# Token rows of the router: from the vector engine to the scalar engine and GpSimd

## The chip, the core and the metric

The program runs on one core of a Trainium2 chip. A core has a matrix engine (PE, TensorE; PEld is its weight loading), a vector engine (DVE), a scalar engine (ACT), GpSimd (POOL) and a queue engine (SP) that here issues nearly all DMA transfers. Each engine works through its own instructions in order and waits on semaphores for the others. The metric is the device time of one execution in microseconds (us); lower is better.

## The reference

Two layers over 256 latent and 256 context tokens of width 1024. Each layer is a norm with modulation, an input projection, three parallel token mixers, an output projection with a residual, and then the part that matters here, a mixture of experts behind a router:

```python
hl = modulate(rms_norm(x, norm2_g[i]), sh2, sc2)            # the token rows h (layer 0: context rows too)
gp = softmax(h @ w_group + b_group);  g_val, g_idx = top_k(gp, 1)
el = (h @ w_expert + b_expert) of the chosen group;  e_val, e_loc = top_k(el, 2)
e_w = softmax(e_val) * g_val
out[e] = (silu(xb @ w_gate[e]) * (xb @ w_up[e])) @ w_down[e]    # for the rows xb sent to expert e
x = x + g2 * (sum over the two experts of e_w * out)
```

32 experts, 1024 x 512 each, three matrices, all in float32, in both layers.

## The kernel before

`layer(l)` writes out both layers. Tokens lie in tiles of 128: NT = 4 tiles in layer 0 (latent and context), NT = 2 in layer 1 (latent only). Expert weights are streamed from HBM through a ring of SBUF places and a pool of 18 tiles of 128 x 1024 (`K4`); what can be loaded before the experts start is loaded early, and after that a place is filled again when PE has read it.

The stretch in question lies between the last residual add and the first expert product:

- `turned(t)`: PE transposes the scaled residual of tile t into a PSUM tile `ht` (pool `P2`, two buffers).
- `lg`, `gmx`, `first_max`, ... to `selb`: the routing steps, some twenty short DVE instructions in a chain: logits, best group, first and second expert, and a 0/1 choice per token and expert.
- `late_mod()`: a modulation product of a later layer, placed in the middle; PE multiplies (line 283, tile `pm`), ACT copies (lines 290 and 306), GpSimd adds (lines 307 to 312). Layer 1 has `own_rows()` at that place instead (PE transposes `xot`, ACT copies `xo`).
- `pp`: PE counts the choices (lines 1218 and 1220); `pos` (DVE, line 1223) is each token's place in its expert; `OH` (line 1303) the one-hot rows of the first four experts.
- `tokens(t)`: DVE makes `h` of tile t, `ht` times the token's norm factor `r2` plus the row `Brow`, in two instructions of 128 x 512 (line 1115); ACT rounds it to `hH` (line 1117). `low(t)`: DVE makes the rest `hL = h - hH` (line 1121).
- `keep_warm(8)`: eight products on PE with no use for their result.
- `gather_all(t)`: PE multiplies `hH` and `hL` of tile t by the one-hot rows (lines 1328 and 1329, tile `pg`); after the last tile the experts' inputs `xg` are complete and the expert products `pgu` (line 1371) start.

From line 1058 on, until `rorder.close()`, the order on PE, DVE, ACT and POOL is that of the code (`rorder`, a manual schedule); SP's order is that of the code throughout. Before the change tile 0's `h` comes right behind `selb` on DVE, and tiles 1 to 3 follow one by one, each behind its transposes, since `ht` has two buffers only.

Of the kernel before, what the change touches and what calls it, by code (L numbers as in the profile page):

```python
# [14 lines left out]
AF = mybir.ActivationFunctionType  # L15
OP = mybir.AluOpType
# [20 lines left out]
def trunk(ctx: ExitStack, tc: tile.TileContext, t_in, rope, out, cfg):  # L37
    nc = tc.nc
    pe, ve, sc, gp, sp = nc.tensor, nc.vector, nc.scalar, nc.gpsimd, nc.sync
# [14 lines left out]
    def K4(name, shape=(128, 1024), dt=F32):  # L54
        return k4.tile(list(shape), dt, tag="k4", name=name)

    def K2(name, shape=(128, 512), dt=F32, tag="t"):
        t = k2[tag].tile([shape[0], 256 if tag == "m" else 512], dt, tag="k2" + tag, name=name)
        n = int(np.prod(shape[1:]))
        t = t[:, :n]  # L60
        if len(shape) == 3:
            t = t.rearrange("p (a b) -> p a b", a=shape[1])
        elif len(shape) == 4:
            t = t.rearrange("p (a b c) -> p a b c", a=shape[1], b=shape[2])
        return t

    def P2(name, dt=F32):
        return ps2.tile([128, 2, 512], dt, tag="p2", name=name)

    def P1(name, dt=F32):  # L70
        return ps1.tile([128, 512], dt, tag="p1", name=name)
# [109 lines left out]
    for i in range(4):  # L181
        t = K4("xtok")
# [146 lines left out]
    def rstd(ssq, n, cnt, name):  # L329

        v = sm.tile([128, n], F32, name=name + "v")
        ve.tensor_scalar(v, ssq, 1.0 / cnt, EPS, op0=OP.mult, op1=OP.add)
        s = sm.tile([128, n], F32, name=name + "s")
        sc.activation(s, v, AF.Sqrt)
        r = sm.tile([128, n], F32, name=name + "r")
        ve.reciprocal(r, s)
        u = sm.tile([128, n], F32, name=name + "u")
        ve.tensor_tensor(u, r, r, op=OP.mult)
        ve.scalar_tensor_tensor(u, u, -0.5, v, op0=OP.mult, op1=OP.mult)
        ve.scalar_tensor_tensor(r, u, 1.5, r, op0=OP.add, op1=OP.mult)  # L340
        return r
# [124 lines left out]
    def layer(l):  # L466
        last = l == DEPTH - 1
        NT = 2 if last else 4
# [439 lines left out]
        def chunked(a):  # L908

            return a.rearrange("t (a p k) -> t a k p", a=2, k=4)  # L910

        def bcast_row(m, s, name, of=lambda a: a):

            t = K4(name)
            p = P2(name)
            for k in range(KC):
                pe.transpose(p[:, k // 4, (k % 4) * 128:(k % 4) * 128 + 128],
                             mod[l][:, m, k, s:s + 1].to_broadcast([128, 128]), ident)
            t_ = t if of is not chunked else t.rearrange("t (a k p) -> t a k p", a=2, k=4)
            sc.copy(t_, of(p.rearrange("p a b -> p (a b)")))  # L920
            return t
# [87 lines left out]
        def weights_of(pr, m, a, e):  # L1009
            return down(a, e, pr) if m == 2 else gate_up(m, a, e, pr)  # L1010
# [5 lines left out]
        def preload_k4(key=None):  # L1016
            key = key or keys.pop(0)
            src = weights_of(*key)
            n = src.shape[1] // 2
            t = []  # L1020
            for b in range(2):
                v = K4("wp", (128, n, src.shape[2]))
                sp.dma_start(v, src[:, n * b:n * b + n])
                t.append(v)
            pre[key] = t
# [27 lines left out]
        for c in order[cfg["wo1"]:]:  # L1053
            t = K4("wo2", (128, 2, 512), F32R)
# [6 lines left out]
        for s in range(NS):  # L1061
            t = K2("wrA", (128, KC, 64))
            gp.tensor_tensor(t, wr, amod[l][:, 1, :, s, None].to_broadcast([128, KC, 64]), op=OP.mult)
            wrA.append(t)
        Brow = []
# [26 lines left out]
        r2 = rstd(ps[:, :NT], NT, D, f"n2{NT}")  # L1092
# [7 lines left out]
        hH, hL, ht, hf = {}, {}, {}, {}  # L1100

        def turned(t, ks=range(KC)):

            if t not in ht:
                ht[t] = P2("ht")
            for k in ks:
                pe.transpose(ht[t][:, k // 4, (k % 4) * 128:(k % 4) * 128 + 128], U(k, 128 * t, 128), ident)

        def tokens(t):
            hf[t] = K4("h")  # L1110
            hH[t] = K4("hH", (128, 1024), F32R)
            p = ht[t].rearrange("p a b -> p (a b)")
            rows = lambda a: a.rearrange("t (a k p) -> t a k p", a=2, k=4)
            for a in range(2):
                ve.scalar_tensor_tensor(rows(hf[t])[:, a], chunked(p)[:, a], r2[:, t:t + 1], rows(Brow[t // 2])[:, a],
                                        op0=OP.mult, op1=OP.add)
            sc.copy(hH[t], hf[t])

        def low(t):
            hL[t] = K4("hL", (128, 1024), F32R)  # L1120
            ve.tensor_tensor(hL[t], hf[t], hH[t].bitcast(F32), op=OP.subtract)
# [3 lines left out]
            pe.transpose(plt[:, 128 * b:128 * b + 128], ls[:, 128 * b:128 * b + 128], ident)  # L1125
        turned(0, range(4, KC))
        turned(1)
        for _ in range(2):
            preload_k4()
        lg = rt.tile([128, 4, 36], F32, name="lg")[:, :NT]  # L1130
# [22 lines left out]
        def own_rows():  # L1153

            for t in range(2):
                xo.append(K4("xo"))
                for a in range(2):
                    p = P1("xot")
                    for k in range(4):
                        pe.transpose(p[:, 128 * k:128 * k + 128], xT[:, 4 * a + k, 128 * t:128 * t + 128], ident)  # L1160
                    sc.copy(xo[t][:, 512 * a:512 * a + 512], p)
# [21 lines left out]
            late_mod()  # L1183
        if last:
            own_rows()
        if last:

            for i in range(cfg["prex"]):
                key = keys.pop(0)
                src = weights_of(*key)  # L1190
                v = xT[:, 4 * i:4 * i + 4].rearrange("p k f -> p (k f)").rearrange("p (k f) -> p k f", f=src.shape[2])
                sp.dma_start(v, src)
                pre[key] = v
# [14 lines left out]
        def keep_warm(n):  # L1208

            p = P1("warm")  # L1210
            for _ in range(n):
                pe.matmul(p[:, 0:256], identb, masks.rearrange("p a b -> p (a b)"), start=True, stop=True)
# [5 lines left out]
                pe.matmul(pp[:, 32 * t:32 * t + 32], tri if u == t else onesb, selb[:, u, :], start=u == 0, stop=u == t)  # L1218
        for u in range(NT):
            pe.matmul(pp[:32, 128:130], selb[:, u, :], onesb[:, 0:2], start=u == 0, stop=u == NT - 1)  # L1220
        tokens(0)
        pos = rt.tile([128, 4, 32], F32, name="pos")[:, :NT]
        ve.scalar_tensor_tensor(pos, pp[:, :32 * NT].rearrange("p (t e) -> p t e", e=32), 1.0, sel, op0=OP.add, op1=OP.mult)

# [319 lines left out]
        onehot()  # L1544
        cnt = rt.tile([32, 1], F32, name="cnt")
        ve.tensor_copy(cnt, pp[:32, 128:129])
        if last:
            g2r = bcast_row(5, 0, "g2r")
        for t in range(1, NT):
            if t > 1:  # L1550
                turned(t)
            tokens(t)
            low(t - 1)
            keep_warm(8)
        low(NT - 1)
        for _ in range(cfg["pre"][l] - 2):
            preload_k4()
        for t in range(NT):
# [102 lines left out]
    for l in range(DEPTH):  # L1661
        layer(l)
# [46 lines left out]
```

## Time and profile before

| what | value |
|---|---|
| median of 3 runs | 1451.4 us (1450.96 to 1451.78) |
| the profiled execution | 1453.9 us, its span 1452.1 us |
| mean granted TensorE clock | 0.983 of full speed |
| PE busy | 1387.6 us, 96% |
| DVE, ACT, POOL busy | 42%, 27%, 5% |
| DMA | 481.86 MB, 332 GB/s mean over the span |

The profile is of one execution. The span runs from the first to the last instruction; what lies around it is 1.8 us. A busy PE is not a PE at its peak. The routing stretch of layer 0 lies at about 284 to 305 us, that of layer 1 at about 965 to 984 us.

### The profile page before, as it was taken

To read this page: it belongs to the slowest core of one execution; us is meant where nothing else is said; L and a number is where in the kernel's file an instruction comes from. 1 tells how busy PE (TensorE), PEld (TensorE's weight loads), DVE (VectorE), ACT (ScalarE), POOL (GpSimd) and SP (SyncE) were. 2 spreads that over 40 slices of the span, in tenths; PEclk is the share of its full clock that TensorE was granted. 3 is DMA by queue.
4 is the path that set the end of the run, shared out by engine and by line. 5 is a ranking of instruction groups with operands and counts; after the bars stand their busy time and mean duration, and the time that the engine had idled before them with its cause. 6 is when DMAs were issued, how large, how long until landed. Compare 5 with 4: busy or idle time off the path is not lost. (4 is left out here: it accounts for less than half of the span.)

```text
span 1452.1 us, 20461 instructions
## 1 busy us (share of the span) xinstructions
PE 1387.6 (96%) x8068; PEld 775.0 (53%) x8068; DVE 610.5 (42%) x1380; ACT 395.0 (27%) x954; POOL 76.3 (5%) x132
## 2 busy tenths in 40 slices
PE   6999999999999999999998998989999999999987
PEld 5777677755445544455434776783434343334332
DVE  3479974353323333233334679853222222122223
ACT  4454775331111111111112565652111111101112
POOL 1212000100000000000001110010000000000000
PEclk9999999999999999999998998999999999999999
DMA  9748303387999999999999591098999999999996
GB/s 352 284 160 292 120 1 133 151 361 315 387 422 417 421 417 417 422 416 419 405 415 388 192 323 44 24 399 326 392 422 421 421 421 422 421 421 419 421 417 255
DMA packets 97556, 481.86 MB, mean 332 GB/s; under 512 B 14084, under 2 KB 22560, under 8 KB 52400
## 3 DMA queue, kind: packets, MB, share of 16 engines
q1 hardware_dynamic: 96720, 478.79, 82.0%
q8 instruction: 66, 1.08, 0.3%
q10 hardware_dynamic: 464, 1.11, 0.2%
q0 software_dynamic: 272, 0.59, 0.1%
q14 instruction: 34, 0.28, 0.1%
HBM read 479.42 MB, written 1.05 MB: 331 GB/s over the span
## 5 line engine op out<-in xcount | busy, mean ns | idle before, releaser
L1371 PE MATMUL pgu<-we,xg 128*64 128x512 f32 x1728 | 403.7, 595 | 12.9 <-DMA we<-in_w_gate_dram 9.3
L1371 PEld LDWEIGHTS pgu<-we,xg 128*64 128x64 f32 x1728 | 132.4, 137 | 270.6 <-issue 223.1
L1425 PE MATMUL py<-we,actT 128*64 128x512 f32 x784 | 178.5, 596 | 0.7 <-ACT actT L1386 0.7
L1380 DVE SCALAR_TENSOR_TENSOR act<-pgu,ws,sil 128x512 f32<-128x512 f32 x32 | 24.0, 751 | 272.6 <-PE pgu L1371 239.5
L1264 DVE SCALAR_TENSOR_TENSOR xT<-pc,mod,xT 128x256 f32<-128x256 f32 x256 | 104.8, 476 | 53.1 <-PE pc L1261 52.5
L1318 ACT COPY xg<-pg 128x256 f32<-128x256 f32 x112 | 36.3, 376 | 296.7 <-PE pg L1314 296.7
L1425 PEld LDWEIGHTS py<-we,actT 128*64 128x64 f32 x784 | 55.4, 137 | 103.2 <-issue 99.9
L1272 DVE TENSOR_TENSOR xo<-xo,pc 128x512 f32<-128x512 f32 x62 | 39.8, 683 | 108.4 <-PE pc L1271 108.4
L1313 PE MATMUL pg<-OH,hH 128*128 128x256 f32 x336 | 83.3, 286 | 0.0
L1314 PE MATMUL pg<-OH,hL 128*128 128x256 f32 x336 | 82.1, 282 | 0.0
L645 DVE SCALAR_TENSOR_TENSOR ca<-gpad,cw,ca 128x512 f32<-128x512 f32 (+1 forms) x120 | 73.2, 610 | 0.7
L1313 PEld LDWEIGHTS pg<-OH,hH 128*128 128x128 f32 x336 | 63.9, 190 | 7.2 <-issue 5.7
L1314 PEld LDWEIGHTS pg<-OH,hL 128*128 128x128 f32 x336 | 64.1, 191 | 0.9
L283 PE MATMUL pm<-wm,scT 128*32 128x256 f32 (+1 forms) x896 | 61.3, 367 | 3.2 <-DMA wm<-in_w_mod_dram 3.1
L1287 DVE TENSOR_TENSOR Yg<-py,g2r 128x512 f32<-128x512 f32 x31 | 21.3, 688 | 100.7 <-PE py L1425 96.4
L1375 ACT ACTIVATE sil<-pgu 128x512 f32<-128x512 f32 x32 | 19.1, 598 | 163.3 <-PE pgu L1371 163.3
L1290 DVE TENSOR_TENSOR YL<-py,YH 128x512 fp32r<-128x512 f32 x32 | 22.1, 690 | 92.8 <-ACT YH L1289 92.8
L1289 ACT CAST YH<-Yg 128x512 fp32r<-128x512 f32 x31 | 19.1, 618 | 141.1 <-DVE Yg L1287 141.1
L1289 ACT CAST YH<-py 128x512 fp32r<-128x512 f32 x32 | 18.7, 585 | 139.0 <-PE py L1425 113.8
L1394 POOL CAST se<-ident 32x128 fp32r<-32x128 f32 x32 | 9.0, 284 | 886.0 <-PE pb L1395 886.0
L1260 PE MATMUL pc<-oht,YH 128*128 128x512 f32 x128 | 53.4, 417 | 1.2 <-ACT YH L1289 1.2
L1371 PE MATMUL pgu<-xT,xg 128*64 128x512 f32 x176 | 46.4, 618 | 5.5 <-DMA xT<-in_w_gate_dram 2.6
(431 smaller groups left out, 2203.5 us busy)
## 6 DMA issues: line engine op xcount, KB each, us to landing
we<-in_w_up_dram SPq DMA_DIRECT2D x102, 1024.0 KB, 10.0
we<-in_w_gate_dram SPq DMA_DIRECT2D x100, 1024.0 KB, 14.8
we<-in_w_down_dram SPq DMA_DIRECT2D x98, 1024.0 KB, 12.3
wm<-in_w_mod_dram SPq DMA_DIRECT2D x44, 1024.0 KB, 8.8
xT<-in_w_down_dram SPq DMA_DIRECT2D x14, 1024.0 KB, 16.2
xT<-in_w_gate_dram SPq DMA_DIRECT2D x10, 1024.0 KB, 19.8
xT<-in_w_up_dram SPq DMA_DIRECT2D x10, 1024.0 KB, 18.8
wp<-in_w_gate_dram SPq DMA_DIRECT2D x8, 1024.0 KB, 10.4
```

The costliest lines, as they stand in the source:

```text
L283: pe.matmul(p[0][32 * q:32 * q + 32], scT[:, kq, :], ws[128 * kq // nr][:, kq % (nr // 128), c:c + n], start=k == 0, stop=k == KC * nq // ...
L645: ve.scalar_tensor_tensor(a, g, wt, a, op0=OP.mult, op1=OP.add)
L1260: pe.matmul(pc, YH[:, 128 * o:128 * o + 128], oht, start=True, stop=False)
L1264: ve.scalar_tensor_tensor(xT[:, o, sl], pc[:, sl], mod[l][:, 5, o, s:s + 1], xT[:, o, sl], op0=OP.mult, op1=OP.add)
L1272: ve.tensor_tensor(xo[t][:, sl], xo[t][:, sl], pc, op=OP.add)
L1289: sc.copy(YH[:rows, sl], py)
L1313: pe.matmul(dst, hH[t][:, 128 * k:128 * k + 128], rhs, start=t == 0, stop=False)
L1314: pe.matmul(dst, hL[t][:, 128 * k:128 * k + 128], rhs, start=False, stop=t == NT - 1)
L1318: sc.copy(xg[e][:, k - 1:k + 1, :], v[:, :, e])
L1371: pe.matmul(p[64 * e:64 * e + 64, :], xg[:, k, 64 * e:64 * e + 64], w_[e](k % 4), start=k == 0, stop=k == KC - 1)
L1380: ve.scalar_tensor_tensor(act, p, ws, sil, op0=OP.mult, op1=OP.mult)
L1425: pe.matmul(py[64 * e:64 * e + 64, h], actT[:, 128 * f + 64 * e:128 * f + 64 * e + 64], wd[e](f % 2)[:, 512 * h:512 * h + 512], start=f == ...
```

## The change

`tokens` no longer makes `h`. A new function `scaled(t)` does: ACT multiplies `ht` by `r2` from PSUM into `h` (two instructions of 128 x 512), and GpSimd adds `Brow` to each half in place. Tiles 0 and 1 are scaled right behind their transposes, before the routing steps, and the transposes of tiles 2 and 3 come there too; tiles 2 and 3 are scaled behind `late_mod`. The rounding to `hH` follows for all tiles on ACT, and DVE makes the four `hL` behind `OH`. One `keep_warm(8)` is left where layer 0 had three (layer 1 had one and keeps it).

```diff
+        def scaled(t):
+
+            hf[t] = K4("h")
+            p = ht[t].rearrange("p a b -> p (a b)")
+            rows = hf[t].rearrange("t (a k p) -> t a k p", a=2, k=4)
+            for a in range(2):
+                sc.activation(rows[:, a], chunked(p)[:, a], AF.Identity, scale=r2[:, t:t + 1])
+                sl = slice(512 * a, 512 * a + 512)
+                gp.tensor_tensor(hf[t][:, sl], hf[t][:, sl], Brow[t // 2][:, sl], op=OP.add)
+
         def tokens(t):
-            hf[t] = K4("h")
             hH[t] = K4("hH", (128, 1024), F32R)
-            p = ht[t].rearrange("p a b -> p (a b)")
-            rows = lambda a: a.rearrange("t (a k p) -> t a k p", a=2, k=4)
-            for a in range(2):
-                ve.scalar_tensor_tensor(rows(hf[t])[:, a], chunked(p)[:, a], r2[:, t:t + 1], rows(Brow[t // 2])[:, a],
-                                        op0=OP.mult, op1=OP.add)
             sc.copy(hH[t], hf[t])
...
         turned(0, range(4, KC))
         turned(1)
+        for t in range(2):
+            scaled(t)
+        for t in range(2, NT):
+            turned(t)
...
         if last:
             own_rows()
+        for t in range(2, NT):
+            scaled(t)
+        for t in range(NT):
+            tokens(t)
...
-        tokens(0)
         pos = rt.tile([128, 4, 32], F32, name="pos")[:, :NT]
...
+        for t in range(NT):
+            low(t)
         if last:
             g2r = bcast_row(5, 0, "g2r")
-        for t in range(1, NT):
-            if t > 1:
-                turned(t)
-            tokens(t)
-            low(t - 1)
-            keep_warm(8)
-        low(NT - 1)
+        keep_warm(8)
```

DVE in layer 0 from the end of the routing steps, before (`rt` stands for the routing tables, `n24r` for `r2`; a name's number is left out):

```order
L1207 CAST selb<-rt 128x128
L1115 SCALAR_TENSOR_TENSOR h<-ht,n24r,Brow 128x512 x2
L1223 SCALAR_TENSOR_TENSOR pos<-pp,rt 128x128
L1303 TENSOR_TENSOR OH<-pos,i_108 128x512 x2
L1546 COPY cnt<-pp 32x1
L1115 SCALAR_TENSOR_TENSOR h<-ht,n24r,Brow 128x512 x2
L1121 TENSOR_TENSOR hL<-h,hH 128x1024
L1115 SCALAR_TENSOR_TENSOR h<-ht,n24r,Brow 128x512 x2
L1121 TENSOR_TENSOR hL<-h,hH 128x1024
L1115 SCALAR_TENSOR_TENSOR h<-ht,n24r,Brow 128x512 x2
L1121 TENSOR_TENSOR hL<-h,hH 128x1024 x2
```

The same place on DVE after the change:

```order
L1219 CAST selb<-rt 128x128
L1234 SCALAR_TENSOR_TENSOR pos<-pp,rt 128x128
L1314 TENSOR_TENSOR OH<-pos,i_108 128x512 x2
L1557 COPY cnt<-pp 32x1
L1125 TENSOR_TENSOR hL<-h,hH 128x1024 x4
```

The eight instructions that made `h` are gone from DVE; the routing steps ahead of `selb` stand as they were.

GpSimd in layer 0 after the change, from the sums of squares (line 977) to the first experts (line 1405, before 1394); before, lines 1117 were not there:

```order
L977 TENSOR_TENSOR sq<-sq 128x512 x5
L1117 TENSOR_TENSOR h<-h,Brow 128x512 x4
L307 TENSOR_TENSOR mod_224<-mod_224,va 128x16
L311 TENSOR_TENSOR amod_226<-mod_224,ones 128x16
L312 TENSOR_TENSOR amod_226<-amod_226,va 128x16
L1117 TENSOR_TENSOR h<-h,Brow 128x512 x4
L1405 CAST se<-ident 32x128 x12
```

Four adds came in ahead of the three small ones of `late_mod`, and four behind them; layer 1 has four in all.

ACT in layer 0 after the change, from the copy of the logits (`ls`) to the copies of the gathered rows (`xg`); before, only lines 1096, 290, 306 and the four roundings stood here:

```order
L1096 COPY ls<-pl 128x256
L1115 ACTIVATE h<-ht,n24r 128x512 x4
L290 COPY ms<-pm 128x256
L306 COPY mod_224<-pm 128x16
L1115 ACTIVATE h<-ht,n24r 128x512 x4
L1121 CAST hH<-h 128x1024 x4
L1344 COPY xg<-pg 128x256 x8
```

The second four scalings stand behind the two copies of `late_mod`, and all four roundings behind those.

## Rows read from the trace of the kernel before

**Rows 1.** The page, part 1: busy us, share of the span, instructions.
```profile
PE 1387.6 (96%) x8068; PEld 775.0 (53%) x8068; DVE 610.5 (42%) x1380; ACT 395.0 (27%) x954; POOL 76.3 (5%) x132
```

**Rows 2.** SP's waits, 240 to 320 us: total us, times, longest.
```profile
SPq L100 <- PE pgu L1371: 16.9, 3, 10.6
```

**Rows 3.** SP's waits, 936 to 1012 us.
```profile
SPq L100 <- PE pgu L1371: 15.5, 3, 9.6
```

**Rows 4.** Windows: stretch, busy PE, PEld, DVE, ACT, POOL, then PE clock, DMA share, GB/s.
```profile
292.00:293.00 1.00, 1.00 (x7) 0.76 (x6) 0.97 (x3) 0.62 (x1) 0.00 (x0) 0.50 0.97 410
...
295.00:296.00 1.00, 1.00 (x9) 0.83 (x8) 1.00 (x2) 0.72 (x1) 0.00 (x0) 0.80 0.97 410
...
309.00:310.00 1.00, 1.00 (x6) 0.29 (x4) 0.90 (x4) 0.80 (x1) 0.00 (x0) 1.00 0.00 0
...
977.00:978.00 1.00, 1.00 (x7) 1.00 (x6) 1.00 (x1) 0.00 (x0) 0.00 (x0) 0.50 0.97 369
...
982.00:983.00 1.00, 1.00 (x7) 0.19 (x4) 0.00 (x0) 0.98 (x2) 0.00 (x0) 1.00 0.01 4
```

**Rows 5.** Timeline, layer 0: start us, us, engine, line, operation [idle before, releaser].
```profile
285.64 0.17 DVE L1166 TENSOR_TENSOR rt<-lg,gmx 128x16 f32<-128x16 f32 x1
285.79 3.66 PE L283 MATMUL pm<-wm,scT 128*32 128x256 f32 x64
...
287.55 0.29 DVE L1167 SCALAR_TENSOR_TENSOR rt<-rt,i 128x128 f32<-128x128 f32 x1
...
290.59 0.17 ACT L306 COPY mod<-pm 128x16 f32<-128x16 f32 x1 [0.70 <-PE pm L297]
...
290.80 0.23 DVE L1207 CAST selb<-rt 128x128 bf16<-128x128 f32 x1
...
291.08 0.18 PE L1218 MATMUL pp<-selb,tri 128*128 128x32 bf16 x1 [0.53 <-DVE selb L1207]
...
292.38 1.05 ACT L1117 CAST hH<-h 128x1024 fp32r<-128x1024 f32 x1 [1.62 <-DVE h L1115]
292.57 1.29 DVE L1303 TENSOR_TENSOR OH<-pos,i 128x512 fp32r<-128x512 f32 x2
...
295.17 1.20 DVE L1121 TENSOR_TENSOR hL<-h,hH 128x1024 fp32r<-128x1024 f32 x1
...
297.56 0.36 PE L1328 MATMUL pg<-OH,hH 128*128 128x256 f32 x1
...
305.40 1.94 PE L1371 MATMUL pgu<-wp,xg 128*64 128x512 f32 x8
```

**Rows 6.** Timeline, layer 1.
```profile
967.07 0.17 DVE L1166 TENSOR_TENSOR rt<-lg,gmx 128x8 f32<-128x8 f32 x1
...
967.92 2.05 ACT L1161 COPY xo<-xot 128x512 f32<-128x512 f32 x4 [2.16 <-PE xot L1160]
...
968.70 0.23 DVE L1167 SCALAR_TENSOR_TENSOR rt<-rt,i 128x64 f32<-128x64 f32 x1
...
971.35 0.19 DVE L1207 CAST selb<-rt 128x64 bf16<-128x64 f32 x1
...
972.91 1.97 PE L917 MATMUL g2r<-ident,mod 128*128 128x128 f32 x8 [0.91 <-DVE h L1115]
...
976.24 0.56 PE L1328 MATMUL pg<-OH,hH 128*128 128x256 f32 x1
```

**Rows 7.** Timeline of GpSimd, 85 to 250 us.
```profile
113.89 5.04 POOL L720 TENSOR_TENSOR qn<-qn,gqk 128x384 f32<-128x384 f32 x4 [4.57 <-issue]
```

**Rows 8.** Line 719, DVE beside Rows 7: ns min/median/max, first to last start.
```profile
L719 DVE TENSOR_TENSOR qn<-qn,rq4r x4: 551/958/1375, 113.2 to 115.4; 128x384 f32<-128x384 f32 x4
```

**Rows 9.** Timeline, 71 to 75 us and 782 to 787 us, GpSimd.
```profile
71.24 3.50 POOL L531 TENSOR_TENSOR wu<-wU,wu 128x256 fp32r<-128x256 f32 x5 [3.27 <-PE pu L537]
...
782.74 4.00 POOL L1572 TENSOR_TENSOR sq<-sq 128x512 f32<-128x512 f32 x3 [10.13 <-ACT sq L419]
```

**Rows 10.** Line 458, DVE reductions, three of them beside the first of Rows 9.
```profile
L458 DVE TENSOR_REDUCE rks<-sqh x8: 279/282/286, 71.7 to 827.6; 128x2 f32<-128x128 f32 x8
```

## The prediction

> **What bounds the kernel now.** I read the page's busy shares first, then SP's waits, then the windows of one microsecond, and last the timeline of the two routing stretches. PE is busy 96% of the span [rows 1], so the end can move only where PE stands still or where its next work comes later. The weight stream does not set the moment at which the experts start: the early loads are done before, the DMA share is 0.00 and 0.01 at 309 and 982 us [rows 4], and the queue then waits for PE to free a place behind the first expert products, 16.9 us in three waits in layer 0 and 15.5 us in three in layer 1 [rows 2, 3]. So all weights of a layer that are not yet loaded start from the first `pgu`, and I count a later `pgu` in full towards the end, in both layers.
>
> What sets the first `pgu`? In layer 0 the routing steps run on DVE from 285.64 to 291.03 us, PE's count `pp` waits for their last result `selb`, the gather starts at 297.56 and `pgu` at 305.40, without a gap between [rows 5]. The gather is 64 products in 7.84 us, 0.12 us each. In layer 1 `selb` is ready at 971.54, PE then counts and waits another 0.91 for DVE's `h` (the transposes `g2r` need the PSUM tile that `h` reads) until 972.91, and the gather starts at 976.24 [rows 6]. Both chains begin with the routing steps on DVE, some twenty instructions, twelve of which read two tensors from SBUF: the tests, the tables and the sums; the reductions read one.
>
> **The change part by part.** *DVE loses* the `h` instructions. What stood on the path was the first pair in layer 1: `g2r` can start with `pp` done, the 0.91 us sooner that its row shows as idle [rows 6], about 0.5 behind `selb`. In layer 0 PE's order held the gather, not DVE alone: it stood behind transposes and `keep_warm` that went from tile to tile with `h`.
>
> *GpSimd gains* eight adds of 128 x 512 in layer 0 and four in layer 1. The nearest row, three adds of this shape in a row, gives 4.00 / 3 = 1.33 us each [rows 9]. The first four of a layer fall on the routing steps, and there the trace has a warning. At 113.9 us GpSimd runs four 128 x 384 products back to back, 5.04 us [rows 7]; beside them DVE's product of two SBUF tensors of the same size takes 1375 ns where it takes 551 alone [rows 8]. The instruction that takes 1375 starts in a GpSimd product and ends behind it: one DVE instruction with two SBUF inputs gets through per GpSimd product. Reductions with one SBUF input are not held: eight of them take 279 to 286 ns, the one at 71.7 us beside five GpSimd products among them [rows 9, 10].
>
> The Trainium skill, "SBUF — State Buffer", section "Who interferes with whom", says the same of the operands, but that issue order decides who blocks: the loser waits for the whole instruction. By that alone DVE's short steps, issued close together, could keep GpSimd out, and the chain would lose nothing (the second rival below); the rows have GpSimd taking its turn each time. I go by the rows.
>
> Layer 0, up to `selb`: `r2` and the first `ht` are there by 285.0, one ACT pass takes about 0.5 us (four copies of this shape from PSUM in 2.05 [rows 6]) and up to 0.7, so the first add starts near 285.7; ACT delivers faster than GpSimd adds, so the four run to 285.7 + 4 x 1.33 = 291.0. In that time DVE does one two-input step per add and the reductions between, some seven steps, which took it from 285.64 to 287.55 before [rows 5]. Delay 291.0 - 287.55 = 3.4 us; `selb` at 294.5. `late_mod` hides under that: PE now has sixteen more transposes ahead of it, which wait for ACT's passes and end at 288.5; `pm` to the copy `mod` took 290.76 - 285.79 = 5.0 [rows 5], so 293.5, before `selb`. Without the delay it would be PE's order that holds `pp`, to 293.5.
>
> Layer 0, from `selb`: `OH` started 1.5 us behind `selb` before, `h` between them included [rows 5], so now at 295.5 to 296. The second four adds start at 294.1, behind `late_mod`'s copy and one ACT pass, and take 5.3 us alone; the two halves of `OH` (1.29 us together) and the first `hL` (1.20) [rows 5] read two SBUF tensors each and take turns with them. At best none is held: `hL` of tile 0 ends at 298.1, since its `hH` (1.05 [rows 5]) stands behind `mod` and four ACT passes of 0.6. At worst all are: 294.1 + 5.3 + 1.3 + 1.2 = 301.9. I take 300.3, in the middle, since some of the adds meet `pos` and the small instructions. The gather waited for nothing at 297.56, so it starts 2.7 us later (0.5 to 4.3); the later `hL` follow every 1.2 us, quicker than a tile's 16 products (1.96 us).
>
> PE's clock: before, PE's waits for `selb` were followed by a granted clock of 0.50, the lower level of 1.2 GHz: at 292 us, on its way back at 295 (0.80), and in layer 1 still at 977, 4 us after `g2r` put PE to work again [rows 4 to 6]. Now PE pauses for some 4 us just ahead of layer 0's gather, which used to start at full clock; 3.5 to 5 us of it at half speed lose half of that, 1.7 to 2.5. I take 1.8 (0 to 2.5).
>
> Layer 0 sums to +4.5 us (0.5 to 6.8).
>
> Layer 1: the first add starts at about 967.1, the four end at 967.1 + 5.3 = 972.4, and DVE has done the seven steps that took it from 967.07 to 968.70 [rows 6]: +3.6, `selb` at 975.2. The adds are over then, nothing else collides. `g2r` starts behind `pp`, 975.6 against 972.91, and with it `keep_warm` and the gather: +2.7 (-0.9 if the chain is not held, 3.5 at most). The gather ran its first products at 0.50 before and does so again.
>
> At nothing I count: ACT's passes in layer 1, which run while DVE is held (in layer 0 they hold `hH`, which is in the bounds above); the two `keep_warm` groups dropped in layer 0 (PE waits there, and the clock's term holds what they kept up); the early weight loads that wait for `late_mod`'s product, 2.7 us later, since the queue was empty at 309 us [rows 4] and the experts that use them come 4.5 later themselves. SP's order is unchanged.
>
> Sum: 4.5 + 2.7 = 7.2 us on the profiled execution's 1453.9, 1461.1. The median of the runs lies 2.5 below that execution, so 1458.6 for the median.
>
> **The rivals.**
> *The engines don't get in each other's way*, or DVE keeps its turn and GpSimd waits. Then layer 0 loses only what PE's order and ACT put in: `pp` at 293.5, the first `hL` at 298.1, +0.5, and up to 1.4 of clock; layer 1 gains 0.9. Sum +1.0: 1452.4, no change that can be told and not slower. Against it: rows 7 and 8. It decides if a layer's chain is held by less than 1.4 us.
> *DVE's relief passes through.* From `selb` to the gather stood 6.5 us in layer 0; `OH` and one `hL` need 2.5, `pp` and `pos` about 1. With `hH` ready the gather could start 3.0 earlier, with 0.9 in layer 1 that is 1447.5. Against it: besides the turns, ACT's order puts the roundings behind `late_mod`.
> *Worse than forecast.* Every two-input step behind the seven is held as well, the eight adds of layer 0 stretch over the whole of `OH` and `hL`, and the gather runs at 0.50 throughout, 7.8 us lost instead of 1.8: up to 1465 and more.
> *The delay is hidden* by a weight stream that is the limit later. But what is not loaded is asked for by PE's progress [rows 2, 3], so a late start is a late stream. With the first rival.
>
> **How the numbers follow.** Forecast 0.68, 1455 to 1461.5 by its own bounds; no collision or hidden 0.18; relief 0.09; worse 0.05. The range for 8 in 10 leaves out the relief below and the worst above: 1450 to 1463. A measurement of this kernel tells a change from none at about 0.2%, 2.9 us. Slower by more than that: the forecast but for its low end, 0.68 x 0.95, and the worst, together 0.70. Faster: 0.08. Between: 0.22.
>
> **What would show it.** In the changed profile the routing steps with two SBUF inputs last over 1 us while GpSimd adds, about four in each layer, and the reductions keep 0.29; `selb` comes 9 us after the first step in layer 0 instead of 5.4, and 8 instead of 4.5 in layer 1; the gather's first products come at a clock of 0.50 in both layers; the stretches of the experts are as long as before, only later. It is wrong if those steps keep 0.3 us, if GpSimd's adds take much longer than 1.3 us instead, or if the first `pgu` is late and the end is not.

## The result, and the profile after

The changed kernel took 1459.89 us (median of 6, 1458.13 to 1463.53), the kernel before 1451.59 on the same chip (median of 6, 1450.96 to 1454.67): a ratio of 1.0061, 95% interval 1.0049 to 1.0074. It is slower, by 8.3 us between the medians; 1458.6 was forecast. The profiled execution of the changed kernel took 1460.6 us, with a span of 1458.9, against 1453.9 and 1452.1 before.

The page, part 1, of the changed kernel (answers to [rows 1]): busy us, share of the span, instructions.

```profile
PE 1387.9 (95%) x8052; PEld 775.2 (53%) x8052; DVE 613.5 (42%) x1368; ACT 402.5 (28%) x966; POOL 94.7 (6%) x144
```

Nothing in that line tells where the time went. The timeline of the two routing stretches does. First GpSimd and DVE in layer 0 (answers to the DVE rows of [rows 5]); the columns are start, duration, engine, line, operation.

```profile
284.81 5.07 POOL L1117 TENSOR_TENSOR h<-h,Brow 128x512 f32<-128x512 f32 x4 [11.79 <-ACT h L1115]
...
293.36 6.91 POOL L1117 TENSOR_TENSOR h<-h,Brow 128x512 f32<-128x512 f32 x4
```

```profile
284.65 0.17 DVE L1174 TENSOR_TENSOR rt<-lg,gmx 128x16 f32<-128x16 f32 x1
284.86 1.24 DVE L1175 SCALAR_TENSOR_TENSOR rt<-rt,i 128x16 f32<-128x16 f32 x1
286.14 0.17 DVE L1177 TENSOR_REDUCE gix<-rt 128x4 f32<-128x16 f32 x1
286.34 1.10 DVE L1182 TENSOR_TENSOR rt<-i,gix 128x128 f32<-128x128 f32 x1
287.48 1.25 DVE L1184 SCALAR_TENSOR_TENSOR rt<-rt,lg 128x128 f32<-128x128 f32 x1
288.77 0.29 DVE L1186 TENSOR_REDUCE m<-rt 128x4 f32<-128x128 f32 x1
289.09 0.94 DVE L1174 TENSOR_TENSOR rt<-rt,m 128x128 f32<-128x128 f32 x1
290.06 0.29 DVE L1175 SCALAR_TENSOR_TENSOR rt<-rt,i 128x128 f32<-128x128 f32 x1
...
293.32 0.23 DVE L1219 CAST selb<-rt 128x128 bf16<-128x128 f32 x1
...
294.55 2.38 DVE L1314 TENSOR_TENSOR OH<-pos,i 128x512 fp32r<-128x512 f32 x2
...
296.92 4.44 DVE L1125 TENSOR_TENSOR hL<-h,hH 128x1024 fp32r<-128x1024 f32 x2
```

The first four adds run from 284.81 to 289.88. In that time four steps with two SBUF inputs last 0.94 to 1.25 us, where the same steps take 0.17 or 0.29 when GpSimd is quiet (the row at 290.06 is the first of these). The two reductions between them keep 0.17 and 0.29. `selb` ends 8.90 us behind the first step; before it was 5.39. Behind it the second four adds meet `OH`, 2.38 us for its two halves instead of 1.29, and the first `hL`, 2.2 us instead of 1.20. There GpSimd loses time too: these four adds take 6.91 us, 1.73 each, where the first four take 1.27.

PE in the same stretch: what it waits for stands in brackets.

```profile
293.60 0.18 PE L1230 MATMUL pp<-selb,tri 128*128 128x32 bf16 x1 [1.29 <-DVE selb L1219]
...
294.12 1.85 PE L1224 MATMUL warm<-masks,identb 128*128 128x256 bf16 x8
295.83 0.58 PE L1339 MATMUL pg<-OH,hH 128*128 128x256 f32 x1
299.19 0.58 PE L1340 MATMUL pg<-OH,hL 128*128 128x256 f32 x1 [2.78 <-DVE hL L1125]
299.57 0.41 PE L1339 MATMUL pg<-OH,hH 128*128 128x256 f32 x1
```

The gather's products take 0.41 us in a row here, 0.28 where PE is at full clock. The windows show the clock (the first of the last three numbers): it falls between 294 and 295 us, while PE runs `keep_warm` behind its waits for `ms` and `selb`, it is at 0.50 while PE waits for `hL`, and it is back between 304 and 305 us.

```profile
294.00:295.00 1.00, 1.00 (x10) 0.75 (x10) 0.74 (x2) 1.00 (x3) 1.00 (x2) 0.60 0.89 344
...
298.00:299.00 1.00, 0.00 (x0) 0.00 (x0) 1.00 (x1) 0.00 (x0) 1.00 (x2) 0.50 1.07 451
...
304.00:305.00 1.00, 1.00 (x9) 1.00 (x8) 0.00 (x0) 0.00 (x0) 0.00 (x0) 0.78 1.05 430
```

Layer 1, PE (answers to the PE rows of [rows 6]):

```profile
980.64 0.21 PE L1230 MATMUL pp<-selb,tri 128*128 128x32 bf16 x1 [5.88 <-DVE selb L1219]
...
980.98 1.97 PE L917 MATMUL g2r<-ident,mod 128*128 128x128 f32 x8
982.74 1.50 PE L1224 MATMUL warm<-masks,identb 128*128 128x256 bf16 x8
984.00 0.36 PE L1339 MATMUL pg<-OH,hH 128*128 128x256 f32 x1
984.20 0.28 PE L1340 MATMUL pg<-OH,hL 128*128 128x256 f32 x1
...
988.00 1.94 PE L1382 MATMUL pgu<-wp,xg 128*64 128x512 f32 x8
```

I measure each layer from its first routing step (the test of `lg` against `gmx`) to its first `pgu`, since everything ahead of the step is the same code. Layer 0 has 24.58 us (284.65 to 309.23) against 19.76, +4.82; layer 1 15.36 (972.64 to 988.00) against 13.97, +1.39. Together +6.2 of the 6.8 by which the span grew. Ahead of layer 0's step the span is 1.0 us shorter; the rest, 1.6, lies behind the two stretches, 1.7 longer between layer 0's `pgu` and layer 1's first step and 0.2 shorter behind layer 1's `pgu`. The first of these took 659.0 to 663.4 us in the profiles of before, after and eleven of the twelve experiments (665.8 in one told below), in no order that follows the changes, so I put such differences down to the single execution.

### The profile page after: what moved, and what is told of

It is laid out like the page before. It is cut to its first block, busy times and chain, and to the rows that moved or that the text cites. A ratio compares the mean times of both kernels' runs of the same rounds, so it can differ in the third digit from the quotient of the medians.

```text
span 1458.9 us, 20445 instructions
## 1 busy us (share of the span) xinstructions
PE 1387.9 (95%) x8052; PEld 775.2 (53%) x8052; DVE 613.5 (42%) x1368; ACT 402.5 (28%) x966; POOL 94.7 (6%) x144
## 4 chain that ended last, share of the span: by engine, by line
PE 30%; DMA 19%; DVE 3%; ACT 1%; issue 1%; SPq 0%; DVEq 0%; POOL 0%; ACTq 0%
DMA we<-in_w_up_dram 12%; PE pgu L1382 9%; PE py L1436 5%; DMA we<-in_w_gate_dram 3%; DMA we<-in_w_down_dram 2%; PE pkv L565 2%; PE pwo L963 1%; PE pq L678 1%; DMA xT<-in_w_up_dram 1%; PE pg L1324 1%; PE pm L283 1%; PE pg L1325 1%; PE py L1412 1%; PE po L864 1%; PE pT L857 1%; PE pat L1395 1%
## 5 line engine op out<-in xcount | busy, mean ns | idle before, releaser
L1272 PE MATMUL pc<-oht,YL 128*128 128x512 f32 x128 | 50.7, 396 | 0.2 <-DVE YL L1301 0.2
```

The source lines that it names most:

```text
L1272: pe.matmul(pc, YL[:, 128 * o:128 * o + 128], oht, start=False, stop=True)
```

## The experiments

Theory T1: GpSimd's adds, because they read two SBUF tensors, hold DVE's steps that do the same, one step per add. Theory T2: the rest of layer 0's delay is PE's clock. Rival R: it is the order of PE or ACT, `late_mod` behind sixteen more transposes above all, and the adds harm nothing. Each run has its own runs of the kernel before on the same chip; the last two columns count from those. Columns: `selb` and the first `pgu` behind the first routing step, in us, from one profile each; the sum of both stretches against the one profile of before; the difference of the medians, and the ratio.

| kernel | selb, layer 0 | pgu, layer 0 | selb, layer 1 | pgu, layer 1 | stretches, sum | time | ratio, 95% |
|---|---|---|---|---|---|---|---|
| before | 5.39 | 19.76 | 4.47 | 13.97 | | | |
| after | 8.90 | 24.58 | 7.95 | 15.36 | +6.2 | +8.3 | 1.0061 (1.0049 to 1.0074) |
| unused adds in before | 8.96 | 23.38 | 8.16 | 16.87 | +6.5 | +6.9 | 1.0046 (1.0029 to 1.0063) |
| unused memsets in before | 5.56 | 19.69 | 4.85 | 14.24 | +0.2 | +0.9 | 1.0001 (0.9989 to 1.0013) |
| no adds | 5.39 | 23.39 | 4.48 | 12.19 | +1.9 | +1.6 | 1.0012 (1.0001 to 1.0023) |
| adds on DVE | 5.40 | 22.48 | 4.49 | 15.02 | +3.8 | +5.6 | 1.0031 (1.0016 to 1.0046) |
| adds cut in halves | 7.70 | 22.46 | 6.92 | 14.65 | +3.4 | +3.4 | 1.0019 (1.0007 to 1.0031) |
| adds held back | 5.40 | 27.02 | 4.47 | 15.33 | +8.6 | +8.5 | 1.0048 (1.0028 to 1.0068) |
| more keep_warm | 8.89 | 22.56 | 7.95 | 15.37 | +4.2 | +6.8 | 1.0043 (1.0028 to 1.0058) |
| order, with adds | 8.89 | 24.45 | 7.96 | 15.58 | +6.3 | +6.7 | 1.0049 (1.0030 to 1.0067) |
| order, no adds | 5.40 | 18.07 | 4.48 | 12.20 | -3.5 | -4.6 | 0.9969 (0.9956 to 0.9982) |
| bias in ACT's copies | 5.39 | 20.31 | 4.46 | 11.95 | -1.5 | +1.9 | 1.0010 (0.9997 to 1.0023) |
| bias in DVE's adds | 5.40 | 17.66 | 4.48 | 12.61 | -3.5 | +5.0 | 1.0031 (1.0019 to 1.0044) |
| shift on PE | 5.40 | 25.91 | 4.40 | 15.64 | +7.8 | +8.7 | 1.0063 (1.0042 to 1.0083) |

**Unused adds in the kernel before.** Nobody waits for these adds and nobody reads what they write.

```diff
+        dum = K2("dum")
+        gp.tensor_copy(dum[:, 0:NT], gmx)
+        for _ in range(4):
+            gp.tensor_tensor(dum, Brow[0][:, 0:512], Brow[0][:, 512:1024], op=OP.add)
```

> The kernel before with four more GpSimd adds of 128 x 512 per layer, which read two SBUF tensors during the routing steps and whose result nobody reads; PE, ACT and DVE have no instruction more. T1: selb comes 3.5 us later in each layer (about 8.9 and 8.0 us behind the first step), the first pgu follows it, and the time is 1456 to 1460 us. Rival R: an engine that shares no data and no buffer with the chain does not hold it; selb at 5.4 and 4.5, time 1451.5.

Measured: `selb` at 8.96 and 8.16, 1457.41 us against 1450.53. T1 holds and R falls in its strong form: adds with no dependence on the chain put 3.6 us into it in each layer, and the first `pgu` follows by 3.6 and 2.9. DVE's rows of layer 0:

```profile
285.31 1.12 DVE L1178 TENSOR_TENSOR rt<-i,gix 128x128 f32<-128x128 f32 x1
286.46 1.32 DVE L1180 SCALAR_TENSOR_TENSOR rt<-rt,lg 128x128 f32<-128x128 f32 x1
...
288.14 0.99 DVE L1170 TENSOR_TENSOR rt<-rt,m 128x128 f32<-128x128 f32 x1
```

**Unused memsets in the kernel before.** The same place, nine instructions that write SBUF and read none.

```diff
+        for _ in range(9):
+            gp.memset(dum, 0.0)
```

> The kernel before with nine GpSimd memsets of 128 x 512 per layer in the same place, which write SBUF but read nothing. If it is the reading of two SBUF tensors on both engines that makes DVE wait, DVE's steps keep 0.3 us, selb stays at 5.4 and 4.5 us behind the first step and the time at 1451 to 1453 us. If any GpSimd instruction that uses SBUF holds DVE, the steps take as long as a memset each and the time rises as with the four adds, to 1456 to 1460 us.

Measured: no change (1451.41 against 1450.53, interval across 1). GpSimd first, then DVE, layer 1:

```profile
963.74 5.18 POOL L1153 MEMSET dum<- 128x512 f32 x9
```

```profile
964.13 0.23 DVE L1178 TENSOR_TENSOR rt<-i,gix 128x64 f32<-128x64 f32 x1
...
967.74 0.64 DVE L1211 CAST selb<-rt 128x64 bf16<-128x64 f32 x1
```

GpSimd is as busy as with the adds (5.18 us), and the two-input steps keep 0.23. So it is what both engines read, not GpSimd's being busy; whether a GpSimd instruction that reads one SBUF tensor holds them no run here shows. One instruction was held: the cast to `selb`, which has one input, 0.64 us instead of 0.19.

**No adds.** The changed kernel with this taken out:

```diff
-                sl = slice(512 * a, 512 * a + 512)
-                gp.tensor_tensor(hf[t][:, sl], hf[t][:, sl], Brow[t // 2][:, sl], op=OP.add)
```

> The changed kernel without GpSimd's adds: the rows stay r2 * ht, so the shift row is left out of the experts' input; PE's order, ACT's passes and DVE's work are those of the changed kernel. Theory T1 (GpSimd's adds hold those steps of DVE that read two tensors from SBUF): selb comes 5.4 us behind the first routing step in layer 0 and 4.5 in layer 1 (changed kernel: 8.90 and 7.95), the steps keep 0.3 us, and the time falls to 1451 to 1454 us, within 0.2% of the kernel before; in layer 0 the count then waits for late_mod instead of selb, to about 8 us behind the first step. Rival R (PE's order or ACT's passes set the start of the gather): selb comes sooner, the first pgu of layer 0 does not, and the time stays at 1457 us or above.

Measured: 1452.12 against 1450.53, `selb` at 5.39 and 4.48. In layer 1 the stretch falls to 12.19, 3.2 below the changed kernel and 1.8 below the kernel before. In layer 0 it falls by 1.2 only, to 23.39: that half of R which I had left standing is true there. PE now stands behind `late_mod` (the count starts at 8.47 us, 3.1 behind `selb`), and 24 of the 64 products of the gather run at the lower clock (0.41 us and more).

**The order of PE and ACT, with the adds and without.** The transposes and passes of tiles 2 and 3 go behind the count, the roundings of tiles 0 and 1 ahead of them.

```diff
-        for t in range(2, NT):
-            turned(t)
...
         pp = P1("pp")
...
+        for t in range(2, NT):
+            turned(t)
+            scaled(t)
+        for t in range(2, NT):
+            tokens(t)
         pos = rt.tile([128, 4, 32], F32, name="pos")[:, :NT]
```

> The changed kernel with GpSimd's adds kept, but the transposes and passes of tiles 2 and 3 behind the count instead of ahead of late_mod, and the roundings of tiles 0 and 1 ahead of them. If the adds alone set selb, it stays at 8.9 us behind the first step in layer 0 and the first pgu at 23 to 25 us; layer 1 as in the changed kernel, 15.4; time 1457.5 to 1460.5 us. If PE's order were what delays layer 0 in the changed kernel, the pgu comes at 21 us or earlier and the time falls to 1456 or below.

> The same order of PE and ACT without GpSimd's adds (the shift row left out of the experts' input). It tells the two holds of layer 0 apart: with both gone, pp stands 5.45 us behind the first step (8.47 with the adds alone gone), the first low part follows at about 8 us, and the first pgu comes at 17 to 20 us, against 23.39 with the adds alone gone and 24.58 in the changed kernel; layer 1 at 12.2. Time 1446 to 1450 us. If something else holds the gather (PE's clock at 0.50 whatever the order), the pgu stays above 21.5 us and the time at 1451 or more.

Measured: with the adds 24.45 us in layer 0 and 1457.93 us; without, 18.07 us and 1446.70 against 1451.25, faster than the kernel before. With the two runs above this is a table of two by two for layer 0's first `pgu`: both holds 24.58, the adds alone 24.45, the order alone 23.39, neither 18.07. Each alone costs 5.3 to 6.4 us and both together 6.5: they lie beside each other, so taking one away shows next to nothing there. The order was moved on PE and ACT together; these runs do not part the two. The two holds can be seen at PE's count. With the adds alone PE waits for `selb`:

```profile
293.95 0.18 PE L1226 MATMUL pp<-selb,tri 128*128 128x32 bf16 x1 [4.02 <-DVE selb L1215]
```

With the order alone (the run without adds) the count comes straight behind `late_mod` and waits for nothing:

```profile
292.15 0.61 PE L297 MATMUL pm<-ident,ms 128*128 128x8 f32 x4 [0.49 <-ACT ms L290]
292.62 0.18 PE L1228 MATMUL pp<-selb,tri 128*128 128x32 bf16 x1
```

With neither it stands right behind `selb`, and the gather is at full clock:

```profile
290.33 0.18 PE L1224 MATMUL pp<-selb,tri 128*128 128x32 bf16 x1 [0.54 <-DVE selb L1213]
...
295.10 0.36 PE L1338 MATMUL pg<-OH,hH 128*128 128x256 f32 x1
295.30 0.28 PE L1339 MATMUL pg<-OH,hL 128*128 128x256 f32 x1
```

**Each add cut in two.** The same work for GpSimd in twice as many instructions.

```diff
-                sl = slice(512 * a, 512 * a + 512)
-                gp.tensor_tensor(hf[t][:, sl], hf[t][:, sl], Brow[t // 2][:, sl], op=OP.add)
+                for b in range(2 * a, 2 * a + 2):
+                    sl = slice(256 * b, 256 * b + 256)
+                    gp.tensor_tensor(hf[t][:, sl], hf[t][:, sl], Brow[t // 2][:, sl], op=OP.add)
```

> The changed kernel with each add of 128 x 512 cut into two of 128 x 256, so GpSimd's work is the same in twice as many instructions. T1 in its narrow form (one DVE step with two SBUF inputs gets through per GpSimd instruction): the held steps take about 0.6 us instead of 0.94 to 1.25, some seven of them, and selb comes about 7.6 us behind the first step in layer 0 (7.2 to 8.0) instead of 8.90, and 6.7 in layer 1 instead of 7.95; time 1457 to 1460 us, since in layer 0 the count waits for late_mod to 8.5 us anyway. If the two engines only share a bandwidth, whatever the cut, selb stays at 8.9 and 8.0 us.

Measured: `selb` at 7.70 and 6.92 (7.6 and 6.7 expected), 1454.47 against 1451.12; the time came out below the range expected, and `late_mod` did not hold the count, which starts at 7.75 us and not at 8.5. GpSimd, then DVE, layer 0:

```profile
283.67 5.84 POOL L1118 TENSOR_TENSOR h<-h,Brow 128x256 f32<-128x256 f32 x8 [11.78 <-ACT h L1115]
```

```profile
285.26 0.70 DVE L1185 SCALAR_TENSOR_TENSOR rt<-rt,lg 128x128 f32<-128x128 f32 x1
...
286.32 0.38 DVE L1175 TENSOR_TENSOR rt<-rt,m 128x128 f32<-128x128 f32 x1
286.74 0.70 DVE L1176 SCALAR_TENSOR_TENSOR rt<-rt,i 128x128 f32<-128x128 f32 x1
```

The held step now lasts about one short add (5.84 / 8 = 0.73 us). A step is held by one GpSimd instruction, not by a share of a bandwidth. Though GpSimd takes 0.8 us longer for the work, the change costs 0.2% in this form instead of 0.6%.

**Adds on DVE, adds held back.** Two ways to keep the adds off the routing steps: on DVE behind `OH`, or on GpSimd behind a small copy of `selb`. Only the new lines are shown.

```diff
+            for a in range(2):
+                sl = slice(512 * a, 512 * a + 512)
+                ve.tensor_tensor(hf[t][:, sl], hf[t][:, sl], Brow[t // 2][:, sl], op=OP.add)
```

```diff
+        gp.tensor_copy(rt.tile([128, 1], BF, name="seen"), selb[:, 0, 0:1])
+        for t in range(NT):
+            for a in range(2):
+                sl = slice(512 * a, 512 * a + 512)
+                gp.tensor_tensor(hf[t][:, sl], hf[t][:, sl], Brow[t // 2][:, sl], op=OP.add)
+            tokens(t)
```

> The changed kernel with the same adds on DVE, behind the one-hot tiles, one tile ahead of the low parts; GpSimd has none of them. T1: selb at 5.4 and 4.5 us behind the first step, the adds cost DVE 0.6 us per 512 columns once the chain to selb is done; 1451 to 1455 us. Rival R: 1457 us or above, as the orders of PE and ACT are those of the changed kernel.

> The changed kernel with GpSimd's adds held back until selb is ready. T1: the routing steps keep 0.3 us and selb comes at 5.4 and 4.5 us behind the first step, but eight adds in a row then end 15.8 us behind it in layer 0 (5.6 + 8 x 1.27), the one-hot tiles and the low parts beside them are held in their turn (over 1 us a piece), and the first pgu comes 22 to 24 us behind the first step (19.76 before, 24.58 in the changed kernel); in layer 1 13.9 to 15 us. Time 1452 to 1457 us. Against T1 would be one-hot halves and low parts at 0.65 and 1.20 us beside running adds.

Measured: 1456.10 against 1450.53, and 1459.57 against 1451.12, both slower than expected. `selb` comes at 5.40 in both. On DVE the adds and low parts of a tile take 2.35 us against 1.96 for its products, so the gather waits for DVE; 1451 to 1455 had not counted that, nor the clock, and with 1456.10 this run alone does not part T1 from R. Held back, the adds delay everything behind them. GpSimd, then DVE, layer 0, and `OH` of layer 1:

```profile
295.33 12.89 POOL L1220 TENSOR_TENSOR h<-h,Brow 128x512 f32<-128x512 f32 x8
```

```profile
298.92 1.23 DVE L1123 TENSOR_TENSOR hL<-h,hH 128x1024 fp32r<-128x1024 f32 x1 [3.52 <-ACT hH L1119]
...
976.74 2.42 DVE L1316 TENSOR_TENSOR OH<-pos,i 128x256 fp32r<-128x256 f32 x2
```

All four low parts of layer 0 keep 1.23 us here: against my expectation they are not the held side. GpSimd is: eight adds take 12.89 us, 1.61 each, and the first `pgu` stands at 27.02 instead of 22 to 24. In layer 1 the halves of `OH` are held as expected, 2.42 us instead of 0.76. DVE comes to each low part after a wait, and to `OH` without one, so I read it that the side that waits depends on how the two engines meet; no run tests that by itself.

**More keep_warm.** `keep_warm(26)` instead of `keep_warm(8)` in layer 0 of the changed kernel.

> The changed kernel with 26 keep_warm products instead of 8 ahead of layer 0's gather, in the 5 us in which PE waits for the first low part. Theory T2 (2.2 us of layer 0's delay are PE's clock, which is at 0.50 when the gather starts, as PE had stood still before): the gather's products start at full clock, 0.28 us each instead of 0.41, the first pgu comes 22.4 us behind the first step instead of 24.58, and the time is 1.5 to 2.2 us below the changed kernel's, 1457.5 to 1458.5 us. If the clock has nothing to do with what PE did in those 5 us, the products stay at 0.41 and the time at 1459.9 us.

Measured: the first `pgu` at 22.56, 2.0 earlier. The clock is back (0.74) while `keep_warm` runs, and the gather is at full clock:

```profile
292.94 4.68 PE L1224 MATMUL warm<-masks,identb 128*128 128x256 bf16 x26
297.37 0.36 PE L1339 MATMUL pg<-OH,hH 128*128 128x256 f32 x1
298.01 0.39 PE L1340 MATMUL pg<-OH,hL 128*128 128x256 f32 x1 [0.27 <-DVE hL L1125]
298.24 0.28 PE L1339 MATMUL pg<-OH,hH 128*128 128x256 f32 x1
```

```profile
296.00:297.00 1.00, 1.00 (x8) 0.82 (x7) 1.00 (x1) 0.50 (x1) 1.00 (x2) 0.74 1.01 426
```

1457.92 us, 2.0 below the changed kernel's 1459.89, as T2 has it; but the two were not timed on one chip, and the intervals of their ratios overlap. The trace carries T2 here, the time alone would not.

**Three versions with the shift row elsewhere.** The run with neither hold leaves the shift row out. Three ways to bring it back without GpSimd: as a bias per feature in ACT's copies of the gathered rows; as the same bias in a broadcast add on DVE; and as a product on PE, which adds shift / r2 to the PSUM rows ahead of ACT's pass. Each moves other work too and changes the number of `keep_warm` products, so they try whole versions and do not test one cause; only the lines that handle the row are shown.

```diff
-                        sc.copy(xg[e][:, k - 1:k + 1, :], v[:, :, e])
+                        for b in range(2):
+                            sc.activation(xg[e][:, k - 1 + b, :], v[:, b, e], AF.Identity, bias=sbias[:, k - 1 + b:k + b])
```

> A version that takes the adds off both engines: the rows are r2 * ht from ACT alone, the shift row of the first batch comes in as a bias per feature in ACT's copies of the gathered experts' input, and only tiles 2 and 3 of layer 0 get the difference of the two batches' rows, on DVE behind the one-hot tiles; late_mod's products stand ahead of the transposes of tiles 2 and 3, g2r's transposes ahead of the count, with 14 and 12 keep_warm products. If selb, PE's order and DVE's rows were what set the gather: selb at 5.4 and 4.5 us behind the first step, first pgu at 17 to 18 us in layer 0 (19.76 before) and 11 to 11.5 in layer 1 (13.97 before), 4 to 5.5 us below the kernel before: 1445 to 1447 us. Rival: the weight stream or ACT's doubled copies take that back later, 1450 us or more.

```diff
+                        ve.tensor_tensor(xg[e][:, k - 1:k + 1, :], v[:, :, e],
+                                         sbias[:, k - 1:k + 1, None].to_broadcast([128, 2, 128]), op=OP.add)
```

> As the version with the shift row as a bias per feature, but three things moved: the bias comes in with DVE's broadcast add in the place of ACT's doubled copies (which had PE wait 7.9 us instead of 0.8 for the activations' transposes in layer 1); the transposes of tiles 2 and 3 and the 16 small products for the bias stand behind the count; the roundings of the first two tiles stand ahead of ACT's other copies. Expected: pp at 5.45 us behind the first step in layer 0 (8.24 in the version with ACT's bias), first pgu 17 to 18.5 us in layer 0 and 11 to 11.8 in layer 1, PE's wait for actT back under 2 us, and 1445 to 1448 us, below the kernel before by 0.2 to 0.4%. Rival: DVE's adds at the experts hold act or split_y, or the weight stream takes the gain back: 1450 us or more.

```diff
+                pe.matmul(ht[t][:, a, :], dg[:, 128 * t:128 * t + 128], Brow[t // 2][:, 512 * a:512 * a + 512], start=False, stop=True)
```

> The order of the run without adds, with the shift row put back where neither DVE nor GpSimd handles it: PE adds it into the PSUM rows before ACT's pass, as a product of a diagonal of 1/r2 with the broadcast row, two products of 128 x 512 per tile (eight in layer 0, four in layer 1), so that ACT's one pass gives r2 * ht + shift; one small reciprocal more on DVE, a small pass per tile more on ACT, and g2r's transposes ahead of the count with 12 keep_warm products. A product of this shape takes 0.24 us at full clock (eight of pgu in 1.94), so PE's share is 2 us in layer 0 and 1 in layer 1, in stretches in which it waits for selb. Expected: selb at 5.4 and 4.5 us behind the first step, first pgu at 18 to 20 us in layer 0 (19.76 before, 18.07 without the row) and 11.3 to 12.3 in layer 1 (13.97 before), and 1446 to 1450 us, faster than the kernel before by 0.1 to 0.35%. Rival: the passes, now behind late_mod, come too late for the gather, or PE's clock falls: 1451 us or more.

None beats the kernel before, though all three were expected to: 1453.06 against 1451.12 (no difference that can be told), 1456.25 against 1451.25, 1460.71 against 1452.00. With ACT's bias the copies double (112 of them become 224 in all but the first group of experts), and `actT`, which PE needs between two experts, queues behind them. PE's waits in layer 1's experts (us in total, times, longest):

```profile
PE py L1443 <- ACT actT L1404: 7.9, 15, 0.6
PE pgu L1389 <- DMA we<-in_w_gate_dram: 5.9, 9, 1.3
```

The kernel before has 0.8 us of the first and 9.3 of the second, so part of the 7.1 more is hidden in waits for weights. With DVE's adds layer 0's stretch is as short as expected (17.66), layer 1's is not (12.61 for 11 to 11.8), and PE's wait for `actT` is gone. But DVE has 20.5 us more work between layer 0's `pgu` and layer 1's first step, that part grows by 4.2 us, and PE waits 2.6 us for a norm of DVE's, 0.4 before. Where the other 2.0 us went stays open, as does why the median of its runs (1456.25) is 3 us above its profiled execution. On PE the price was wrong:

```profile
291.81 3.68 PE L1099 MATMUL ht<-Brow,dg 128*128 128x512 f32 x8
```

Four products take 3.68 us, 0.92 each, not 0.24: the row I had priced by has half the columns of weights and counts each product twice. They stand ahead of the count, which starts 9.66 us behind the first step.

## Why the prediction was right, point by point

- *DVE's steps wait for GpSimd's adds, one per add; reductions do not.* Right. Four steps of 0.94 to 1.25 us in layer 0, four of 0.94 to 1.19 in layer 1, reductions at 0.16 to 0.29. The unused adds show that nothing but the adds is needed, the memsets that it is their reading, the halved adds that the unit is one instruction. The Trainium skill, "SBUF — State Buffer", section "Who interferes with whom", has it that a two-input DVE instruction contends with GpSimd where that reads SBUF and not where it only writes; the adds and the memsets agree, 0.94 to 1.32 us against 0.23.
- *The adds start near 285.7 and take 1.33 us each; seven steps are done by their end.* They started 0.16 us behind the first step (0.06 forecast) and took 1.27 each; DVE's seventh step ended 0.15 us behind the last of them. `selb` came at 8.90 us (9 forecast) and 7.95 (8 forecast).
- *`late_mod` hides under that.* Right as far as the count goes: PE waits 1.29 us for `selb` behind it. The prediction also said that PE's order would hold the count without the delay; the run without adds has it so, at 8.47 us. What it did not see is how much that hold is worth alone. For the rival in which the engines do not get in each other's way it gave layer 0 +0.5 and up to 1.4 of clock; the run without adds has +3.6 there, and -1.8 instead of -0.9 in layer 1. The two errors cancel in part: the rival's sum was +1.0, the stretches of that run have +1.9 and its median +1.6.
- *Layer 0's gather starts 2.7 us later (0.5 to 4.3).* Right: the first product with a low part stands 14.54 us behind the first step, 2.6 later than 11.92 (the start of the gather before).
- *PE's clock costs layer 0 1.8 us (0 to 2.5).* Right in the size: from the first product with a low part to `pgu` are 10.04 us, where the gather took 7.84, and with 26 `keep_warm` products the stretch is 2.0 shorter. One thing is otherwise than forecast: the clock does not fall in the pause ahead of the gather, which begins at 296.4, but between 294 and 295. It fell in the kernel before too (0.50 at 292) and was on its way back at 295 [rows 4]; in the changed kernel it is not, and the run with 26 products, which fill the pause, has it on its way back at 296 (0.74), ahead of the gather. Layer 0 as a whole: +4.82 for 4.5.
- *Layer 1 loses 2.7 us.* The term that was mis-sized: +1.39. `selb` is 3.48 later (3.6 forecast; its own terms, 972.4 less 968.70, give 3.7) and `g2r` follows it 0.39 us behind instead of 1.37 (0.9 sooner forecast), but from `selb` to the gather are 3.41 us instead of 4.70, and the gather then runs at full clock at once, 4.00 us instead of 4.80. The step that failed is "the gather ran its first products at 0.50 before and does so again". In both kernels the clock falls to 0.50 while PE waits for `selb`, and comes back behind `g2r`. The windows of the kernel before, then of the changed one (the first of the last three numbers is the clock):

```profile
971.00:972.00 1.00, 0.40 (x5) 0.28 (x5) 0.93 (x4) 0.00 (x0) 0.00 (x0) 0.62 1.02 430
978.00:979.00 1.00, 1.00 (x10) 1.00 (x9) 0.28 (x3) 0.00 (x0) 0.00 (x0) 0.97 1.00 410
```

```profile
976.00:977.00 1.00, 0.00 (x0) 0.00 (x0) 0.96 (x2) 1.00 (x3) 1.00 (x2) 0.93 0.93 369
983.00:984.00 1.00, 1.00 (x8) 0.78 (x7) 1.00 (x2) 1.00 (x1) 0.00 (x0) 0.66 1.00 410
```

  Between these windows every one has 0.50. Before, `g2r` starts at 972.91, soon behind the fall, and the clock is back some 5 us later, in the middle of the gather. Now the fall is 4 us ahead of `g2r` (980.98), and the clock is back some 2.7 us behind its start, before the gather. The later `selb` thus gave back, in the clock, part of what it took; why PE's work brought the clock back sooner here no run settles.
- *The experts' stretches are as long as before, only later.* Right: 470.90 us for 471.06 in layer 1, with 9.6 us of PE's waits for `in_w_gate` weights there where 9.3 stood before; in layer 0 +1.7, inside what the single executions differ by.
- *DVE's relief passes through: 1447.5.* Ruled out for the change. Without the adds, so without the shift row, and with the other order 1446.70 was measured, so there was time to gain. Against the kernel before that run gains 1.7 us in layer 0 (18.07 for 19.76) and 1.8 in layer 1; the adds and the order cost 6.5 and 3.2 on top of it.

The sum was 7.2, the span grew by 6.8, the median by 8.3 (7.1 to 10.7 by the interval of the ratio). The two stretches carry 6.2 of that: layer 0 was forecast 0.3 too low, layer 1 1.3 too high. The other 2.1 us of the median no row explains; they are of the size by which executions of one kernel differ (1447.6 to 1455.6 for the kernel before over all chips). That 1458.6 came so near 1459.89 is therefore in part luck; that the change is slower, and the terms of layer 0, were forecast rightly.

## What to carry to other kernels

Work put on an idle GpSimd is not free for a chain of small DVE steps beside it: every step with two SBUF inputs may wait for a whole GpSimd instruction that reads SBUF, so put such work where DVE reduces or reads PSUM (`pos`, one input from each, kept 0.29 us beside the second four adds), or cut it into short instructions. When an order and a collision both hold the same start, removing one shows almost nothing; take both away at once before judging either. A wait on PE can also keep its clock low in what follows, 2.0 us here, and products that fill the wait buy that back.

## What the runs showed of the hardware that was not expected

- Either side can wait. In the routing steps DVE waits and the adds keep 1.27 us; beside `OH` and the first `hL` of the changed kernel both lose, and the adds take 1.73; with the adds behind `selb`, layer 0's low parts keep 1.23 us and the adds grow to 1.61.
- A one-input cast waits for memsets: `selb` took 0.64 and 0.39 us beside them instead of 0.19 and 0.23, while two-input steps went free. The same section of the Trainium skill's page "SBUF — State Buffer" names casts among the operations that can take the shared ports when their operands meet its conditions; these two rows agree.
- Adds of 128 x 256 take 0.73 us beside DVE's steps, more than half of 1.27: the halves cost GpSimd 15% more and DVE 1.2 us less.
